# Two moves at the end of a decoder step: the transposition of the sampled parts' weights one slot later, and the last norm's spread written to two banks

## The chip, the cores and the metric

The kernel runs on one core of a Trainium2 chip. The metric is device microseconds of one execution, from the first instruction to the last transfer. Three executions of the kernel before took 937.68, 939.5 and 942.25 us, median 939.5 us. One further execution was profiled; it took 936.85 us.

The engines are named as the profile names them: PE multiplies matrices and writes its sums to banks of PSUM, DVE and ACT work on tiles and may read those banks, POOL works on tiles in SBUF, SP issues most transfers. Each engine works through its own instructions in their order and waits for others by semaphores.

## The reference

One step of a hybrid decoder on a prompt of 512 tokens and on 32 sampled tokens (8 sequences of 4). A first layer is a Mamba-2 mixer; a second is an attention mixer with three dilation groups that all read one shared K/V. What the change touches is the end of the second layer: the merging of the three groups' results by a softmax over their log-sum-exps, the gate, the output projection, the residual and the final norm.

```python
def dilated_mixer(h, attend, biases, g_norm, w_in, w_out):
    u = rmsnorm(h, g_norm) @ w_in
    q, gate = ...
    for g in range(N_DIL_GROUPS):
        o, lse = attend(q[:, :, g], biases[g], ...)
        ...
    w = jax.nn.softmax(jnp.stack(lses, axis=0), axis=0)
    o = jnp.sum(w[..., None] * jnp.stack(outs, axis=0), axis=0)
    y = o.reshape(b, l, ATT_WIDTH) * jax.nn.silu(gate)
    return y.astype(h.dtype) @ w_out

hp = hp + dilated_mixer(hp, attend_p, ...)      # the prompt
hs = hs + dilated_mixer(hs, attend_s, ...)      # the sampled tokens
y_prompt = rmsnorm(hp, final_norm)
y_sample = rmsnorm(hs, final_norm)
```

## The kernel before, in words

Prompt and sampled tokens stand side by side as 544 columns; the 1024 features are eight tiles of 128 rows. A product in full precision is made of three passes: operands are split into a high part (ACT) and a low part (DVE), and PE adds high x high, high x low and low x high. `mm` (line 146) and `transpose` (line 149) are the helpers through which nearly all PE work goes, so PE's rows are told apart by their tiles.

In the last stage a list of `units` is worked through: `attend(h, n)` for a head and a quarter of the prompt, `sample(h, q)` for a head and half of the sampled sequences, and near the end `combine()`. All three are generators; each `yield` ends one piece. Unit u's first piece is built in round u, its second in round u + 2, its third in u + 3, its fourth in u + 4, so other units' pieces stand between. After each round `run(n)` takes n matmuls from a `filler` that keeps PE busy with independent work: first the input projection for the queries and the gate (`pair_filler`, tiles `pa` and `pb`, inputs `bq`, weights `whi` and `wlo`), then the output projection (`out_proj`, inputs `yh` and `yl`, weights `wo`). The order in which instructions are built, with some marked urgent, is what a scheduler turns into the order on each engine; where an instruction lands in DVE's order thus follows from where it is built, and from what the scheduler puts ahead of it.

The gate's evacuation (`gate_evac`) is a chain through one spare tile `kv`: DVE L1213 reads the product's bank, ACT L1215 makes a Tanh, DVE L1220 (and L1222 for the sampled columns) and L1227 multiply, and ACT L1328 and DVE L1329 split the result into `yh` and `yl`. `wo` tiles are split by ACT L205 and DVE L206.

`combine` merges the sampled tokens' three groups. Piece one takes logarithms, transposes `lse`, makes the softmax in `qpad` (DVE L1484 to L1501, ACT L1496). Piece two transposes the weights on PE into the bank `lp2` (shown as `lp<-ident,qpad`), copies them to `sbt` (DVE L1507) and spreads them (L1508). Piece three makes sixteen small products `oc` in eight pairs, with two matmuls of the filler after each pair (`run(OCN)`, OCN is 2), and copies `oc` to `ys`, whose product with the gate is split last.

`out_proj` goes over the columns in two parts of 272 and over eight row tiles `m`; for each, 24 matmuls, then the residual (DVE L1610), a square (ACT L1611), a running sum (POOL L1613) and the gain (ACT L1614). When a part is done, its sums over the rows are made on PE (`ms`), and the reciprocal root is spread to all rows by a product of ones with a diagonal matrix (`rp`). For the last part `norm_last` does this: DVE multiplies six of the eight row tiles by the bank itself, in three pieces (L1592), each sent off by SP; ACT copies the bank to SBUF (L1585), POOL multiplies the other two tiles by that copy (L1588), and ACT's queue sends them (L1589).

Banks come from two pools in rotation: three for `pa` and `pb`, five (`pss`) for everything else here.

Of the kernel before, what the change touches and what calls it, by code (L numbers as in the profile page):

```python
# [127 lines left out]
def tile_yoco_step(  # L128
# [6 lines left out]
    nc = tc.nc  # L135
# [3 lines left out]
    def pin(ins):  # L139
        if pinned[0]:  # L140
            tc.keep_in_program_order(ins)
# [3 lines left out]
    def mm(*a, **k):  # L145
        pin(nc.tensor.matmul(*a, **k))  # L146

    def transpose(*a):
        pin(nc.tensor.transpose(*a))  # L149
# [7 lines left out]
    def half(name, dt=F32, shape=(128, 4, T)):  # L157
        return slab.tile(list(shape), dt, name=name, tag="s")

    def pj(name, cols=512):  # L160
        return psum.tile([128, cols], F32, name=name, tag="pj", bufs=3)

    def pss(name, shape=(128, 512)):
        return psum.tile(list(shape), F32, name=name, tag="ss", bufs=5)
# [15 lines left out]
    ones = const.tile([128, 128], F32, name="ones")  # L180
# [353 lines left out]
    for i in range(2):  # L534
        for j in range(2):
            p = pj("pa")
# [12 lines left out]
    dgs = tm[:, 1200:1584].rearrange("p (a b) -> p a b", b=128)  # L549
# [99 lines left out]
    def bc(ap, n):  # L649
        return ap[:, :, None].to_broadcast([ap.shape[0], ap.shape[1], n])  # L650
# [240 lines left out]
    def run(n):  # L891
        for _ in range(n):
            if next(fill, 0) == 0:
                return
# [237 lines left out]
    for k in range(4):  # L1132
        b1, b2 = (wk.tile([128, T], F32, name="hb", bufs=2) for _ in range(2))
# [343 lines left out]
    def combine():  # L1477
        nc.scalar.activation(lsm, lsm, AF.Ln)
        nc.vector.tensor_tensor(lse, lsm, lse, op=ALU.subtract)
        lp = pss("lp")  # L1480
        transpose(lp[0:16, 0:128], lse, ident)
        ltr = qpad[0][0:16]
        lt = ltr[:, 0:4, :]
        nc.vector.tensor_copy(lt.rearrange("p a b -> p (a b)"), lp[0:16, 0:128])  # L1484
        lv = lt[:, :, 0:12].rearrange("p j (g t) -> p j t g", t=TS)
        lgv = lt[:, :, 0:12].rearrange("p j (g t) -> p g j t", t=TS)
        red = ltr[:, 4, :].rearrange("p (a j t) -> p a j t", a=2, t=TS)
        mxg, sm_ = red[:, 0], red[:, 1]

        def all_groups(a):  # L1490
            return a[:, None, :, :].to_broadcast([16, 3, 4, TS])

        nc.vector.tensor_reduce(out=mxg, in_=lv, axis=AX.X, op=ALU.max)
        for g in range(3):
            nc.vector.tensor_tensor(lgv[:, g], lgv[:, g], mxg, op=ALU.subtract)
        nc.scalar.activation(lt[:, :, 0:12], lt[:, :, 0:12], AF.Exp)  # L1496
        nc.vector.tensor_reduce(out=sm_, in_=lv, axis=AX.X, op=ALU.add)
        nc.vector.reciprocal(sm_, sm_)
        for g in range(3):
            nc.vector.tensor_tensor(lgv[:, g], lgv[:, g], sm_, op=ALU.mult)  # L1500
        nc.vector.memset(lt[:, :, 12:32], 0.0)  # L1501
        yield
        lp2 = pss("lp2")
        transpose(lp2[:, 0:16], lt.rearrange("p a b -> p (a b)"), ident[0:16, 0:16])
        cmw = sbt[:, 0:272].rearrange("p (a b) -> p a b", b=16)
        ws, cm = cmw[:, 16, :], cmw[:, 0:16, :]
        nc.vector.tensor_copy(ws, lp2[:, 0:16])  # L1507
        nc.vector.tensor_tensor(cm, sel[:, None, :].to_broadcast([128, 16, 16]), bc(ws, 16), op=ALU.mult)  # L1508
        yield
        oc = pss("oc", (128, ATH, 2, 16))  # L1510
        for h in range(ATH):
            for q in range(2):
                mm(oc[:, h, q, :], o_s[:, q, h, :], cm[:, 2 * h + q, :], start=True, stop=True)
                if q:
                    run(OCN)
        nc.scalar.copy(y_s, oc.rearrange("p h q c -> p h (q c)"))
        sample_y()

    def sample_y():
        if len(late_smp) == 1:  # L1520
            nc.vector.scalar_tensor_tensor(y_s, y_s, 0.5, u_s, op0=ALU.mult, op1=ALU.mult)
            for i in range(2):
                split2(y_h[i][:, :, 0:NS], y_l[i][:, :, 0:NS], y_s[:, 4 * i:4 * i + 4, :])
        late_smp.append(1)
# [13 lines left out]
    def out_proj():  # L1538
        h2 = [half("h2"), half("h2")]
        for i in range(2):  # L1540
            dma(h2[i], h1d[:, 4 * i:4 * i + 4, :])
        e = half("e").rearrange("p a b -> p (a b)")
        accs, tmps = [e[:, HB * i:HB * i + HB] for i in range(2)], [e[:, HB * (2 + i):HB * (3 + i)] for i in range(2)]
        dgs = [e[:, HB * (4 + i):HB * (5 + i)] for i in range(2)]
        wos = {}

        def get(m):
            if m < KD and m not in wos:
                wos[m] = load_w(wo[m], half("wo", F32R, (128, 2, 8, 128)) if m < KD - 2 else None)

        def norm_sum(part, c0, c1):
            n = c1 - c0
            b0s = (0, 128, n - 128) if n > 256 else (0, 128)
            ms = pss("ms")
            for s_ in (0, 1):
                for b, b0 in enumerate(b0s):
                    mm(ms[:, b:b + 1], (accs, tmps)[s_][part if s_ == 0 else 1][:, b0:b0 + 128], inv_d,
                       start=s_ == 0 and b == 0, stop=s_ == 1, skip_group_check=True)
            return ms, n, b0s

        def norm_mul(sums, part, c0, c1):
            ms, n, b0s = sums
            rs = rstd_fin(ms, n, b0s, dgs[part])
            for m in range(0, KD, 2):
                hm = h2[m // 4][:, m % 4:m % 4 + 2, c0:c1]
                nc.vector.tensor_tensor(hm, hm, rs[:, None, 0:n].to_broadcast([128, 2, n]), op=ALU.mult)
                dma(yT[:, m:m + 2, c0:c1], hm)


        def norm_last(sums, part, c0, c1):  # L1570
            ms, n, b0s = sums
            sd = const.tile([128, 5], F32, name="sd", bufs=2)
            nc.scalar.activation(sd[:, 0:3], ms[:, 0:3], AF.Sqrt, bias=epst)
            nc.vector.reciprocal(sd[:, 0:3], sd[:, 0:3])
            idle = pss("idle")
            for _ in range(6):
                mm(idle[:, 0:128], ones, ones, start=True, stop=True)
            dg, rp = dgs[part], pss("rp")
            nc.scalar.activation(dg[:, 128:256], ident, AF.Copy, scale=sd[:, 1:2])
            nc.vector.tensor_scalar(dg[:, 0:128], ident, sd[:, 0:1], None, op0=ALU.mult)  # L1580
            nc.vector.tensor_scalar(dg[:, 256:n], ident[:, 384 - n:128], sd[:, 2:3], None, op0=ALU.mult)
            for b0, b1 in ((0, 128), (128, n)):
                mm(rp[:, b0:b1], ones, dg[:, b0:b1], start=True, stop=True, skip_group_check=True)
            rs = tmps[0][:, 0:n]
            nc.scalar.copy(rs, rp[:, 0:n])  # L1585
            for m in range(KD - 2, KD):
                hm = h2[m // 4][:, m % 4, c0:c1]
                nc.gpsimd.tensor_tensor(hm, hm, rs, op=ALU.mult)  # L1588
                nc.scalar.dma_start(yT[:, m, c0:c1], hm)  # L1589
            for m in range(0, KD - 2, 2):  # L1590
                hm = h2[m // 4][:, m % 4:m % 4 + 2, c0:c1]
                nc.vector.tensor_tensor(hm, hm, rp[:, None, 0:n].to_broadcast([128, 2, n]), op=ALU.mult)  # L1592
                dma(yT[:, m:m + 2, c0:c1], hm)

        get(0)
        parts = ((TH, T), (0, TH))
        for part, (c0, c1) in enumerate(parts):
            n = c1 - c0
            acc = accs[part]
            for m in range(KD):  # L1600
                get(m + 1)
                p = pj("pa")
                yield from proj_steps(p, [wos[m]], y_h, y_l, c0, c1, order=(0, 1, 2, 3, 5, 7, 6, 4))
                if part and m == 0:
                    sums = norm_sum(0, *parts[0])
                if part and m == 1:
                    norm_mul(sums, 0, *parts[0])
                hm = h2[m // 4][:, m % 4, c0:c1]
                sq = acc if m == 0 else tmps[m % 2]
                nc.vector.tensor_tensor(hm, p[:, 0:n], hm, op=ALU.add)  # L1610
                nc.scalar.activation(sq[:, 0:n], hm, AF.Square)  # L1611
                if 0 < m < KD - 1:
                    nc.gpsimd.tensor_tensor(acc[:, 0:n], acc[:, 0:n], sq[:, 0:n], op=ALU.add)  # L1613
                nc.scalar.activation(hm, hm, AF.Copy, scale=g_f[:, m:m + 1])  # L1614
        norm_last(norm_sum(1, *parts[1]), 1, *parts[1])

    ahead = [0]
# [130 lines left out]
```

## Time and profile before

| | |
|---|---|
| median of three runs | 939.5 us (937.68 to 942.25) |
| the profiled execution | 936.85 us, span 935.0 us |
| granted PE clock, mean | 0.995 |
| PE busy | 914.6 us, 98% of the span |
| DVE / ACT / POOL busy | 689.0 / 482.8 / 197.5 us |
| first output projection matmul | 873.34 us |
| last `rp` matmul ends | 928.29 us |

A row of a timeline gives start, duration, engine, line, operation and tiles (out<-in), and in brackets how long the engine had stood idle and what ended that. A row of a table by windows gives the stretch, its length, then the busy time and number of instructions of PE, PE's weight loads, DVE, ACT and POOL, then the granted PE clock (1.00 is full), the share of the DMA engines' time in use and GB/s. A row of waits gives the engine and tile that waited, for what, the total in us, how often, and the longest.

### The profile page before, as it was taken

How to read it: one execution, taken by the hardware profiler on the slowest of the kernel's cores; microseconds unless marked ns; L12 is line 12 of the kernel's file. 1: busy time of each engine (PE TensorE's matmuls, PEld its weight loads, DVE VectorE, ACT ScalarE, POOL GpSimd, SP SyncE). 2: the span in 40 equal slices, each digit the busy share in tenths (PEclk: the TensorE clock that was granted, in tenths of full speed). 3: DMA queues.
4: the chain of work that ended last, by engine and by line, in shares of the span. 5: the costliest groups of instructions: out<-in, count | busy, mean ns of one | idle time of the engine just before them, and what ended most of it. 6: DMA issues, size and time to landing. Idle time of an engine off the chain costs nothing.

```text
span 935.0 us, 21902 instructions
## 1 busy us (share of the span) xinstructions
PE 914.6 (98%) x8667; PEld 844.4 (90%) x8667; DVE 689.0 (74%) x1458; ACT 482.8 (52%) x1074; POOL 197.5 (21%) x295
## 2 busy tenths in 40 slices
PE   8999998999999999999999999999999999999996
PEld 8999887889888889999999999988888888888996
DVE  6997999989899889655489436866677766777732
ACT  6568655655655645322255213555555555557642
POOL 2133555644743733111101000000000000000021
PEclk9999999999999999999999999999999999999999
DMA  8225355255454443536287556767867868785411
GB/s 282 92 74 140 125 197 202 85 169 163 151 192 167 172 142 113 170 95 222 94 268 226 181 171 194 256 205 252 265 206 241 271 228 265 242 262 179 153 48 48
DMA packets 75950, 168.49 MB, mean 180 GB/s; under 512 B 19462, under 2 KB 37208, under 8 KB 75336
## 3 DMA queue, kind: packets, MB, share of 16 engines
q1 hardware_dynamic: 71464, 154.60, 50.3%
q10 hardware_dynamic: 3312, 9.75, 2.7%
q0 software_dynamic: 1072, 2.74, 1.1%
q8 instruction: 68, 1.11, 0.5%
q14 instruction: 34, 0.28, 0.1%
HBM read 141.14 MB, written 25.93 MB: 179 GB/s over the span
## 4 chain that ended last, share of the span: by engine, by line
PE 87%; DVE 5%; DMA 4%; ACT 2%; POOL 1%; issue 1%; SPq 0%; DVEq 0%; ACTq 0%
PE pa L146 35%; PE pb L146 30%; PE sp L146 3%; PE so L146 3%; PE pv L146 2%; PE s L146 2%; PE yd L146 1%; PE csp L146 1%; PE w L149 1%; PE ptp L149 1%; PE yo L146 1%; PE xp L149 1%; DMA ssmS<-s 1%; DVE co L638 1%; PE yos L146 1%; DMA kc<-ck 1%
## 5 line engine op out<-in xcount | busy, mean ns | idle before, releaser
L205 ACT ACTIVATE whi<-wraw 128x1024 fp32r<-128x1024 f32 x69 | 72.9, 1057 | 99.3 <-PE pb L146 68.7
L206 DVE TENSOR_TENSOR wlo<-wraw,whi 128x1024 fp32r<-128x1024 f32 x69 | 86.7, 1256 | 45.0 <-ACT whi L205 44.4
L146 PE MATMUL pa<-bq,whi 128*128 128x272 f32 x512 | 103.2, 296 | 0.0
L146 PE MATMUL pb<-nh,whi 128*128 128x288 f32 x280 | 83.7, 299 | 3.9 <-ACT cb L340 3.9
L146 PE MATMUL pb<-nl,whi 128*128 128x288 f32 x280 | 84.0, 300 | 0.0
L146 PE MATMUL pb<-nh,wlo 128*128 128x288 f32 x280 | 83.6, 299 | 0.0
L146 PEld LDWEIGHTS pa<-bq,whi 128*128 128x128 f32 x512 | 81.3, 189 | 0.9
L146 PE MATMUL pa<-nh,whi 128*128 128x256 f32 x280 | 80.6, 288 | 0.0
L146 PE MATMUL pa<-nl,whi 128*128 128x256 f32 x280 | 80.1, 286 | 0.0
L146 PE MATMUL pa<-nh,wlo 128*128 128x256 f32 x280 | 79.5, 284 | 0.0
L146 PE MATMUL pb<-bq,whi 128*128 128x272 f32 x384 | 77.1, 295 | 0.5 <-DVE kv L1213 0.5
L146 PE MATMUL pa<-bq,wlo 128*128 128x272 f32 x256 | 74.2, 290 | 0.0
L638 DVE SCALAR_TENSOR_TENSOR co<-cb,cvp,co 128x568 f32<-128x568 f32 x72 | 65.9, 917 | 0.8 <-ACT co L636 0.5
L146 PEld LDWEIGHTS pb<-bq,whi 128*128 128x128 f32 x384 | 60.8, 189 | 1.6 <-DVE kv L1213 0.8
L1449 POOL COPY lse<-mxs 128x1 f32<-128x1 f32 x16 | 4.6, 289 | 267.3 <-DVE mxs L1447 267.3
L1272 ACT ACTIVATE whi<-wraw 128x512 fp32r<-128x512 f32 x64 | 40.1, 626 | 36.8 <-PE pb L146 16.9
L146 PEld LDWEIGHTS pb<-nh,whi 128*128 128x128 f32 x280 | 53.1, 190 | 5.0 <-ACT cb L340 4.2
L146 PEld LDWEIGHTS pb<-nl,whi 128*128 128x128 f32 x280 | 53.0, 189 | 4.4 <-issue 4.4
L146 PE MATMUL pb<-bq,wlo 128*128 128x272 f32 x192 | 55.4, 289 | 0.0
L146 PEld LDWEIGHTS pb<-nh,wlo 128*128 128x128 f32 x280 | 53.1, 190 | 2.2 <-issue 2.2
L146 PEld LDWEIGHTS pa<-nh,whi 128*128 128x128 f32 x280 | 53.3, 190 | 1.9 <-issue 1.7
L146 PEld LDWEIGHTS pa<-nl,whi 128*128 128x128 f32 x280 | 53.3, 190 | 1.4 <-issue 1.4
(401 smaller groups left out, 2858.4 us busy)
## 6 DMA issues: line engine op xcount, KB each, us to landing
wraw<-w_in SPq DMA_DIRECT2D x40, 512.0 KB
kc<-ck SPq DMA_DIRECT2D x32, 640.0 KB
vc<-cv SPq DMA_DIRECT2D x32, 640.0 KB
wraw<-wb SPq DMA_DIRECT2D x32, 512.0 KB
s<-s SPq DMA_DIRECT2D x16, 512.0 KB
m<-aed SPq DMA_DIRECT2D x16, 512.0 KB
ssmS<-s ACTq DMA_DIRECT2D x16, 512.0 KB
wraw<-w_out SPq DMA_DIRECT2D x16, 512.0 KB
```

Of the source, the lines that this page charges most:

```text
L146: pin(nc.tensor.matmul(*a, **k))
L149: pin(nc.tensor.transpose(*a))
L205: a = nc.scalar.activation(hi, raw, AF.Copy)
L206: b = lo_eng.tensor_tensor(lo, raw, f32(hi), op=ALU.subtract)
L638: nc.vector.scalar_tensor_tensor(o, cb[:, k:k + n], cvp[:, ti, k:k + 1], o, op0=ALU.mult, op1=ALU.add)
L1272: nc.scalar.activation(hi, src[p][j], AF.Copy)
L1449: nc.gpsimd.tensor_copy(lse[:, i16:i16 + 1], mx[:, 2:3])
```

## The change

`combine` yields once more between its first and its second piece, so the transposition is built one round later, and with it all that follows in `combine`. In `norm_last` the spread is written twice, to a bank `rp` for DVE and to a bank `rc` for ACT; ACT copies from `rc`.

```diff
         nc.vector.memset(lt[:, :, 12:32], 0.0)
         yield
+        yield
         lp2 = pss("lp2")
         transpose(lp2[:, 0:16], lt.rearrange("p a b -> p (a b)"), ident[0:16, 0:16])
...
-            dg, rp = dgs[part], pss("rp")
+            dg, rp, rc = dgs[part], pss("rp"), pss("rc")
...
-            for b0, b1 in ((0, 128), (128, n)):
-                mm(rp[:, b0:b1], ones, dg[:, b0:b1], start=True, stop=True, skip_group_check=True)
+            for p in (rp, rc):
+                for b0, b1 in ((0, 128), (128, n)):
+                    mm(p[:, b0:b1], ones, dg[:, b0:b1], start=True, stop=True, skip_group_check=True)
             rs = tmps[0][:, 0:n]
-            nc.scalar.copy(rs, rp[:, 0:n])
+            nc.scalar.copy(rs, rc[:, 0:n])
```

What this does to the order. First PE, where the transposition was: it stood between the gate product `pa` of `bq_6930` and `pv` of the attention.

```order
 L146 MATMUL pa<-bq_6930,whi 128x272 x2
 L146 MATMUL pa<-bq_6930,wlo 128x272
-L149 MATMUL lp_11406<-ident,qpad_7044 128x16
 L146 MATMUL pv<-kv,pt 128x128 x2
 L146 MATMUL pv<-kv,pt 32x128 x4
```

It is now behind the attention's transposes `ptp`, and the rest of the gate products follow it without interruption. PE, some rows further, with the change (the products of `bq_6932` are the last of the gate's; `yh`, `yl` with `wo` are the output projection's first):

```order
L149 MATMUL ptp<-ident,s 32x128
L149 MATMUL lp_11453<-ident,qpad_7044 128x16
L146 MATMUL pb<-bq_6933,wlo 128x272
...
L146 MATMUL pa<-bq_6932,wlo 128x272
L146 MATMUL pa<-yh,wo 128x272
L146 MATMUL pa<-yl,wo 128x272
L146 MATMUL pa<-yh,wo 128x272 x2
L146 MATMUL oc<-sbt,os 128x16 x2
L146 MATMUL pa<-yl,wo 128x272
```

Before, the first `oc` stood directly behind `ptp`, and the eight pairs were spread over the last gate products; now they are spread over the first block of the output projection. The number of matmuls between them is the same.

Then DVE, at the copy and the spreading of the weights (L1507 and L1508 before, L1508 and L1509 with the change). With the change:

```order
L206 TENSOR_TENSOR wo<-wraw,wo 128x1024
L1220 SCALAR_TENSOR_TENSOR kv<-kv 128x272
L1329 TENSOR_TENSOR yl<-y_7037,yh 128x272
L1213 SCALAR_TENSOR_TENSOR kv<-pa,sums 128x272
L1227 SCALAR_TENSOR_TENSOR y_7037<-y_7037,kv 128x272
L1329 TENSOR_TENSOR yl<-y_7037,yh 128x384
L1508 COPY sbt<-lp_11453 128x16
L1220 SCALAR_TENSOR_TENSOR kv<-kv 128x240
L1222 SCALAR_TENSOR_TENSOR us<-kv 128x32
L1329 TENSOR_TENSOR yl<-y_7037,yh 128x272
L1227 SCALAR_TENSOR_TENSOR y_7037<-y_7037,kv 128x240
L1509 TENSOR_TENSOR sbt<-csts,sbt 128x256
```

Before, both stood fifteen rows and more higher, next to the attention's L1380, ahead of the last three gate evacuations; now the copy stands within the last evacuation (L1213 of `pa`, L1220, L1222, L1227) and the spreading behind it.

Last the end of the program on DVE, with the semaphores that each row waits for, before and with the change:

```order
L1592 TENSOR_TENSOR h_11510<-h_11510,rp 128x2x272 [waits Activation_49]
L1592 TENSOR_TENSOR h_11510<-h_11510,rp 128x2x272
L1592 TENSOR_TENSOR h_11511<-h_11511,rp 128x2x272
```

```order
L1594 TENSOR_TENSOR h_11487<-h_11487,rp 128x2x272 [waits PE_49]
L1594 TENSOR_TENSOR h_11487<-h_11487,rp 128x2x272
L1594 TENSOR_TENSOR h_11488<-h_11488,rp 128x2x272
```

DVE waited for ACT's copy of the same bank; now it waits for PE's last matmul into `rp`. On PE two matmuls into `rc` follow those into `rp`, and ACT's copy waits for them.

## The prediction

> **What bounds the kernel now.** I read the page first, then its chain of waits, then PE's waits, and only then the timelines of the stretch that the change touches.
>
> ```profile
> PE 914.6 (98%) x8667; PEld 844.4 (90%) x8667; DVE 689.0 (74%) x1458; ACT 482.8 (52%) x1074; POOL 197.5 (21%) x295
> PE 87%; DVE 5%; DMA 4%; ACT 2%; POOL 1%; issue 1%; SPq 0%; DVEq 0%; ACTq 0%
> ...
> PE lp L149 <- DVE qpad L1500: 0.7, 1, 0.7
> PE pb L146 <- DVE kv L1213: 0.5, 1, 0.5
> ...
> 879.37 22.15 PE pa L146 x176
> ```
>
> PE is busy 98% of the span, and 87% of the chain is PE. So a microsecond in which PE stands still costs a microsecond, and a microsecond saved on another engine is worth nothing unless PE waited for it. Of PE's waits, the one of 0.7 us is for `qpad` at L1500: that is the transposition of the weights, which the change moves. The other, 0.5 us for L1213, stands beside it. The last row, from the chain, gives the pitch of a 128x272 matmul, 22.15 / 176 = 0.126 us, and shows that after 879 us PE runs on without a gap, so whatever is lost or won before is carried to the end.
>
> **The transposition, what it removes.** PE and DVE in order of time, before the change:
>
> ```profile
> 861.89 0.29 PE L146 MATMUL pa<-bq,wlo 128*128 128x272 f32 x1
> 862.88 0.20 PE L149 MATMUL lp<-ident,qpad 16*128 16x16 f32 x1 [0.70 <-DVE qpad L1500]
> 863.01 1.07 PE L146 MATMUL pv<-kv,pt 128*128 128x128 f32 x12
> ...
> 869.02 0.29 PE L146 MATMUL pb<-bq,wlo 128*128 128x272 f32 x1
> ```
>
> Without `lp2` here `pv` would start one pitch after 861.89, at 862.02, and it starts at 863.01: 0.99 us are gained. Its inputs allow that: the copies into `pt` (L1391, L1392) are released by transposes before this place. One slot later `lp2` costs PE its own 863.01 - 862.88 = 0.13 us and no wait, as DVE finished `qpad` long before. Net -0.86 us. The 0.5 us for L1213 stays: that matmul adds to the bank that L1213 reads.
>
> **What the move puts in its place.** `oc`, the sixteen small products that use the weights, now begins four matmuls into the output projection, and its first one waits for DVE's L1509 (L1508 before), which spreads the transposed weights into `sbt`. DVE works in order, and L1509 now stands behind the last gate's evacuation. What stands ahead of it, and how long that took:
>
> ```profile
> 869.35 1.06 ACT L205 ACTIVATE wo<-wraw 128x1024 fp32r<-128x1024 f32 x1 [0.98 <-PE pb L146]
> ```
> ```profile
> 863.68 0.16 DVE L1507 COPY sbt<-lp 128x16 f32<-128x16 f32 x1
> 863.79 0.21 DVE L1380 TENSOR_SCALAR mx<-mx 128x1 f32<-128x1 f32 x1
> 863.92 0.42 DVE L1508 TENSOR_TENSOR sbt<-csts,sbt 128x256 f32<-128x256 f32 x1
> ...
> 870.44 1.23 DVE L206 TENSOR_TENSOR wo<-wraw,wo 128x1024 fp32r<-128x1024 f32 x1 [0.30 <-ACT wo L205]
> 871.58 0.43 DVE L1220 SCALAR_TENSOR_TENSOR kv<-kv 128x272 f32<-128x272 f32 x1
> 871.94 0.43 DVE L1329 TENSOR_TENSOR yl<-y,yh 128x272 fp32r<-128x272 f32 x1
> 873.53 0.44 DVE L1213 SCALAR_TENSOR_TENSOR kv<-pa,sums 128x272 f32<-128x272 f32 x1 [1.17 <-PE pa L146]
> ...
> 875.60 0.40 DVE L1227 SCALAR_TENSOR_TENSOR y<-y,kv 128x240 f32<-128x240 f32 x1
> 875.92 0.42 DVE L1521 SCALAR_TENSOR_TENSOR ys<-ys,us 128x256 f32<-128x256 f32 x1
> ```
>
> The clock for all of it is the end of the last `pb` product, 869.02 + 0.29 = 869.31. From there:
>
> - ACT's L205 splits the second `wo` tile, and DVE's L206 begins at 870.44: 1.13 us later.
> - L206, L1220, L1329 take 871.58 - 870.44 = 1.14, then 0.36, and about 0.35 for the next of the same form, so L1213 can begin 1.85 us after L206. Before, it waited 1.17 us more for PE; now PE is early, and DVE is what is late.
> - From L1213 to the end of L1227, 875.92 - 873.53 = 2.39 us (in it an ACT Tanh that waits for L1227 and is waited for by L1220). L1508 adds 0.11 (863.79 - 863.68), L1509 0.42.
>
> Sum: 1.13 + 1.85 + 2.39 + 0.11 + 0.42 + 0.03 for the semaphore = 5.93 us after that end. PE reaches the first `oc` much sooner: twelve matmuls of the last gate product and four of the projection follow, so its next start would be 869.02 + 17 x 0.126 = 871.16, or 1.85 us after the same end. PE loses 5.93 - 1.85 = 4.08 us, shown as a wait of about 3.9, since a last matmul's 0.29 us end is drawn past its pitch. Behind that `oc` all of PE stands, the rest of the projection included. The eight pairs of `oc` and sixteen matmuls between them are as many as before. Later covers hold: the split of the third `wo` tile follows the end of the first projection block, as before, so it moves with PE.
>
> Bounds: if ACT's L205 or DVE's L206 kept their old place in time the wait would be shorter by the 0.98 us that ACT waited for PE; I take 3.1 as the low end. If every DVE hand-over costs 0.03 us more, ten of them, 4.4. I take 4.08. Stretch: -0.86 + 4.08 = +3.2 us.
>
> **The clock behind the wait.** The trace holds one wait of that length, at 160.5 us, and shows what follows it. Windows, with the granted clock behind the five engines, and PE's rows:
>
> ```profile
> 164.40:165.00 0.60, 0.55 (x4) 0.55 (x5) 0.60 (x2) 0.60 (x4) 0.60 (x1) 1.00 0.00 0
> 165.00:165.50 0.50, 0.50 (x5) 0.50 (x5) 0.47 (x3) 0.26 (x1) 0.50 (x3) 0.86 0.00 0
> 165.50:166.00 0.50, 0.50 (x4) 0.50 (x3) 0.50 (x1) 0.35 (x1) 0.50 (x2) 0.50 0.00 0
> 168.50:168.75 0.25, 0.25 (x3) 0.25 (x3) 0.25 (x2) 0.25 (x2) 0.09 (x1) 0.50 0.00 0
> 168.75:169.00 0.25, 0.25 (x3) 0.13 (x1) 0.25 (x1) 0.25 (x3) 0.00 (x0) 0.95 0.00 0
> 933.25:933.50 0.25, 0.00 (x0) 0.00 (x0) 0.00 (x0) 0.00 (x0) 0.00 (x0) 0.73 0.98 357
> ```
> ```profile
> 160.23 0.28 PE L146 MATMUL pa<-nh,wlo 128*128 128x256 f32 x1
> 164.45 0.40 PE L146 MATMUL pb<-nh,whi 128*128 128x288 f32 x1 [3.94 <-ACT cb L340]
> 164.69 0.30 PE L146 MATMUL pb<-nl,whi 128*128 128x288 f32 x1
> 164.82 0.29 PE L146 MATMUL pb<-nh,wlo 128*128 128x288 f32 x1
> 166.06 0.45 PE L146 MATMUL pb<-nh,whi 128*128 128x288 f32 x1
> 166.30 0.45 PE L146 MATMUL pb<-nl,whi 128*128 128x288 f32 x1
> ```
>
> About 0.9 us after PE had resumed, the clock went to 0.50 at 165.36 (0.86 = 1 - 0.28 / 2 of that row) and came back at 168.77: 3.41 us at half, in which a matmul came every 0.24 us where 0.13 stood before. The drop at the end, at 933.36, lies 768.0 us later, 225 x 3.413, so such windows follow a fixed beat. The one that brought the first drop, 161.95 to 165.36, was 27% busy; the one from 926.53 to 929.95, half busy up to the last `rp` near 928.3, brought none. A wait of 3.9 us leaves one of its windows at best 43% busy, at some phases empty. So I expect a drop in most executions. At half rate the 3.41 us lose up to 1.7 us; where the drop falls inside the wait, part of it is lost on an idle PE, down to 0.7. I take 1.4, bounds 0 and 3.4 (two windows).
>
> The Trainium skill (TensorE: Matmul & The Clock Gate, section "What's actually happening") says that half rate is what PE falls to after at least one idle window of about 3.4 us. The length agrees with the 3.41 measured here; that the window must be idle does not, since the one at 161.95 was 27% busy. Read strictly, it would let a wait of 3.9 us drop the clock in about (3.9 - 3.41) / 3.41, one phase in seven, and the time would be that of the second rival below.
>
> **The last norm's spread.**
>
> ```profile
> 928.37 0.39 ACT L1585 COPY e<-rp 128x272 f32<-128x272 f32 x1 [1.06 <-PE rp L146]
> 928.79 1.98 DVE L1592 TENSOR_TENSOR h<-h,rp 128x544 f32<-128x544 f32 x3 [1.45 <-ACT e L1585]
> 928.83 1.48 POOL L1588 TENSOR_TENSOR h<-h,e 128x272 f32<-128x272 f32 x2 [5.46 <-ACT e L1585]
> 929.54 1.67 SPq L1593 DMA_DIRECT2D yT<-h  x3
> 927.81 0.48 PE rp L146 x4
> 930.25:930.50 0.25, 0.00 (x0) 0.00 (x0) 0.25 (x1) 0.00 (x0) 0.06 (x1) 1.00 0.21 74
> 930.50:930.75 0.25, 0.00 (x0) 0.00 (x0) 0.25 (x1) 0.00 (x0) 0.00 (x0) 1.00 1.00 357
> ```
>
> DVE's three multiplications waited for ACT's copy out of the same bank; with a bank of its own DVE waits for `rp` alone and starts at about 928.37, 0.42 us earlier. The second spread, `rc`, is as many rows again, 0.48 us (row of the chain), so the copy and POOL start 0.48 us later. That is covered: from 930.4 to past 933.25 the DMA engines are full with the results, so what counts is when the first transfer starts, and that is SP's at 929.54, which follows DVE's first piece. POOL's two small parts then come at about 930.1 and 930.8 (928.83 + 0.48, and 0.74 for each), while the queues are still full. Gain 0.42 us; bounds 0 (POOL's last part ends all) and 0.45.
>
> **The sum.** +3.2 + 1.4 - 0.4 = +4.2 us. The profiled execution took 936.85 us for a span of 935.0, so 941.0 us. It lies 2.65 us under the median of the runs shown, 939.5; against that median the forecast is 939.5 + 4.2 = 943.7 us, or +0.44%. About 0.5%, 4.7 us, is what a measurement of this kernel can tell from no change.
>
> **The rivals.**
>
> 1. *Slower beyond doubt: the clock stays down for two windows.* Where the beat splits the wait in the middle, both windows hold about 1.95 us of it, and the second may keep the clock low too. For it: the 27% row. Against: after 164.45 one busy window was enough. Price +3.2 + 3.4 - 0.4 = +6.2 us, 945.7; it passes 0.5% once more than 1.9 us go to the clock.
> 2. *The wait, but no drop.* For it: the half-busy window near 928. Against: the drop at 165.36. +3.2 - 0.4 = +2.8 us, 942.3.
> 3. *Not slower: PE never waits for L1509.* If DVE were done by the time PE is there, only the gains stand: -0.86 - 0.42 = -1.3 us, 938.2. For it: DVE is 74% busy, and has 1.17 us of slack ahead of L1213. Against: the sum above, 5.93 against 1.85; DVE would have to be 4 us ahead of every row quoted.
> 4. *The second bank does nothing*, because POOL's late start ends the run: the sum is 0.4 us higher, 944.1. The full DMA rows speak against it.
>
> **How the numbers follow.** Forecast (one drop) 55%, rival 1 15%, rival 2 17%, rival 3 4%, rival 4 9%. The likeliest gives 943.7. The runs of before lie 4.6 us apart, so a median can be off by some 1.5 us: low 940.5 (rival 2 less that), high 947 (rival 1 plus it). Slower by over 0.5%: a third of the forecast (0.19), most of rival 1 (0.13), a little of 2, and half of rival 4 (0.04), 0.38 in all. Faster by over 0.5%: 0.02. Within: 0.60.
>
> **What would show it.** In the new profile: no wait of PE for `qpad`; one wait of PE of 3.5 to 4.3 us at `oc`, for DVE `sbt` L1509, near 870 us; behind it a window of 3.41 us at clock 0.5; DVE's L1594 starting with `rc`, no longer behind ACT. If there is no wait at `oc`, the middle part is wrong; if it is there and the clock stays at 1.00, the clock term is; if the first result transfer does not start about 0.4 us sooner after the last `rp`, the last part is.

## The result and the profile after

The changed kernel takes 947.95 us (median of five executions, 945.6 to 950.35) against 939.5 us before (five executions beside it, 937.55 to 942.25): a ratio of 1.0096, 95% interval 1.0077 to 1.0116. It is slower by 8.4 us, where +4.2 was forecast, and above the upper end of the range, 947. The profiled execution took 947.61 us for a span of 945.8, against 936.85 and 935.0.

First the new wait of PE in the changed kernel (engine and tile, what it waited for, total us, times, longest):

```profile
PE oc L146 <- DVE sbt L1509: 3.9, 1, 3.9
```

The wait for `qpad` is gone from the list and one of 3.9 us stands in its place, as the prediction had it. DVE's and PE's timelines show how it comes about, and how long the stage then lasts:

```profile
870.42 1.23 DVE L206 TENSOR_TENSOR wo<-wraw,wo 128x1024 fp32r<-128x1024 f32 x1 [0.30 <-ACT wo L205]
...
872.27 0.44 DVE L1213 SCALAR_TENSOR_TENSOR kv<-pa,sums 128x272 f32<-128x272 f32 x1
...
874.64 0.42 DVE L1509 TENSOR_TENSOR sbt<-csts,sbt 128x256 f32<-128x256 f32 x1
```
```profile
857.76 0.28 PE L149 MATMUL lp<-ident,lse 128*16 128x128 f32 x1
...
869.00 0.29 PE L146 MATMUL pb<-bq,wlo 128*128 128x272 f32 x1
...
870.86 0.41 PE L146 MATMUL pa<-yh,wo 128*128 128x272 f32 x2
875.21 0.76 PE L146 MATMUL oc<-sbt,os 128*128 128x16 f32 x4 [3.94 <-DVE sbt L1509]
...
876.41 0.87 PE L146 MATMUL oc<-sbt,os 128*128 128x16 f32 x4
877.71 0.87 PE L146 MATMUL oc<-sbt,os 128*128 128x16 f32 x4
...
890.39 0.27 PE L149 MATMUL op<-ident,on 128*128 128x128 f32 x1
```

From the end of the last `pb` product, 869.29, the first `oc` starts 5.92 us later; 5.93 was worked out. What was not foreseen is the pitch behind it: one step of the alternation (two `oc` products, shown as four instructions, and two matmuls of the projection) takes 877.71 - 876.41 = 1.30 us. Before, the same step took 0.70 us:

```profile
856.20 0.28 PE L149 MATMUL lp<-ident,lse 128*16 128x128 f32 x1
...
867.76 0.52 PE L146 MATMUL oc<-sbt,os 128*128 128x16 f32 x4
868.45 0.51 PE L146 MATMUL oc<-sbt,os 128*128 128x16 f32 x4
...
879.10 0.27 PE L149 MATMUL op<-ident,on 128*128 128x128 f32 x1
```

The windows of the changed kernel, cut at the beat of 3.413 us, show why (after the stretch and its length: busy time and instructions of PE, its weight loads, DVE, ACT and POOL; then the granted clock):

```profile
872.08:875.49 3.41, 0.28 (x3) 0.31 (x3) 3.27 (x11) 1.15 (x3) 0.00 (x0) 1.00 0.53 157
875.49:878.91 3.42, 3.42 (x17) 3.42 (x17) 0.12 (x1) 0.00 (x0) 0.00 (x0) 0.50 0.00 1
878.91:882.32 3.41, 3.41 (x18) 3.41 (x17) 0.00 (x0) 0.00 (x0) 0.00 (x0) 0.50 0.00 0
882.32:885.73 3.41, 3.41 (x16) 3.41 (x17) 0.17 (x1) 0.37 (x1) 0.00 (x0) 0.50 0.00 0
885.73:889.15 3.42, 3.42 (x22) 2.81 (x21) 1.10 (x4) 1.43 (x5) 0.00 (x0) 0.50 0.00 0
889.15:892.56 3.41, 3.41 (x29) 3.41 (x29) 2.67 (x3) 3.02 (x4) 0.00 (x0) 1.00 0.11 18
```

The clock is at half for four windows, 13.65 us, and not for one. PE is drawn busy all through them, and its waits show nothing there: only the granted clock and the pitch tell of the loss. In the kernel before, the same mix of products ran at full clock:

```profile
868.51:871.93 3.42, 3.42 (x31) 3.42 (x31) 2.72 (x5) 2.12 (x4) 0.00 (x0) 1.00 0.44 156
```

**Where the 10.8 us of the two spans lie.** From the transposition of `lse` to the last `op` the kernel before took 879.10 - 856.20 = 22.90 us, the changed one 890.39 - 857.76 = 32.63: 9.73 us more. Of these the stretch is 3.2 by the forecast, so 6.5 go to the clock; half of 13.65 would be 6.8. (The run with the covered wait, below, measures the stretch without a drop, and leaves 6.3.) Ahead of `lse`, where the change touches nothing, the profiled execution after ran 857.76 - 856.20 = 1.56 us late. The rest is a gain at the end, in PE's, DVE's and SP's rows:

```profile
938.81 0.64 PE L146 MATMUL rp<-e,ones 128*128 128x128 f32 x4
939.28 0.63 PE L146 MATMUL rc<-e,ones 128*128 128x128 f32 x4
939.49 1.98 DVE L1594 TENSOR_TENSOR h<-h,rp 128x544 f32<-128x544 f32 x3 [0.98 <-PE rp L146]
...
940.28 1.62 SPq L1595 DMA_DIRECT2D yT<-h  x3
```

DVE starts 0.68 us after the first `rp`, no longer behind ACT. Before, it started 1.15 us after it (928.79 against `rp` at 927.64, in a row quoted further down), so 0.47 us are won there. The first result transfer starts 1.47 us after `rp` instead of 1.90 (929.54 in the prediction), and to the end of the span it is 945.8 - 938.81 = 7.0 us instead of 7.4.

### The profile page after: what moved, and what is told of

Its sections match the earlier page's. It is cut to its first block, busy times and chain, and to the rows that moved or that the text cites. A ratio compares the mean times of both kernels' runs of the same rounds, so it can differ in the third digit from the quotient of the medians.

```text
span 945.8 us, 21909 instructions
## 1 busy us (share of the span) xinstructions
PE 923.0 (98%) x8671; PEld 852.0 (90%) x8671; DVE 687.5 (73%) x1458; ACT 483.5 (51%) x1074; POOL 196.7 (21%) x295
## 4 chain that ended last, share of the span: by engine, by line
PE 87%; DVE 5%; DMA 3%; ACT 2%; issue 1%; POOL 1%; SPq 0%; POOLq 0%; DVEq 0%; ACTq 0%
PE pa L146 35%; PE pb L146 30%; PE sp L146 3%; PE so L146 3%; PE s L146 2%; PE pv L146 2%; PE yd L146 1%; PE csp L146 1%; PE yo L146 1%; PE ptp L149 1%; PE xp L149 1%; PE w L149 1%; PE yos L146 1%; DVE co L638 1%; DMA kc<-ck 1%
```

## The experiments

**Two theories on the four windows.** Theory 1: the clock is kept down by what runs behind the wait. The `oc` products pass 16 columns for each load of 128x128 weights, so little passes through the array while PE is drawn busy; behind the wait of 160 us, on which the forecast was modelled, only wide products follow. Theory 2: the number of windows follows from the wait itself, its length or its place on the beat. A third question is whether the whole loss comes from the late place of the spread L1509 in DVE's order. In all diffs the changed kernel is the starting point unless something else is said.

### One part alone: the transposition

```diff
-            dg, rp, rc = dgs[part], pss("rp"), pss("rc")
+            dg, rp = dgs[part], pss("rp")
...
-            for p in (rp, rc):
-                for b0, b1 in ((0, 128), (128, n)):
-                    mm(p[:, b0:b1], ones, dg[:, b0:b1], start=True, stop=True, skip_group_check=True)
+            for b0, b1 in ((0, 128), (128, n)):
+                mm(rp[:, b0:b1], ones, dg[:, b0:b1], start=True, stop=True, skip_group_check=True)
...
-            nc.scalar.copy(rs, rc[:, 0:n])
+            nc.scalar.copy(rs, rp[:, 0:n])
```

> The transposition one slot later, the last spread in one bank as before. If the whole loss comes from the place of the transposition: the change with both parts measured +8.4 us over the kernel before (947.95 against 939.5), its second part is priced at -0.4, so +8.8 us, about 948.3, with PE's wait of 3.9 us at the first oc, and behind it about 13.6 us at half clock. If the second spread bank were part of the loss: less than +8 us.

Measured: 946.69 us against 938.0, ratio 1.0087 (1.0055 to 1.012), +8.7 us by the medians. The wait is 3.9 us again. In the profiled execution the clock stays down for five windows, 878.35 to 895.42; before them the end of the wait, then the first and the fourth:

```profile
874.94:878.35 3.41, 0.18 (x2) 0.00 (x0) 3.41 (x11) 1.09 (x4) 0.00 (x0) 1.00 0.62 207
878.35:881.77 3.42, 2.72 (x12) 2.75 (x13) 0.96 (x3) 0.40 (x1) 0.00 (x0) 0.50 0.00 1
...
888.59:892.01 3.42, 3.42 (x20) 2.81 (x21) 0.42 (x1) 1.14 (x4) 0.00 (x0) 0.50 0.00 0
```

So the loss is the transposition's, as far as these intervals tell. Here the wait lies otherwise on the beat: the first `oc`, at 879.05, starts 0.70 us behind the drop, in the change (875.21) 0.28 us ahead of it. The number of windows is five instead of four. Both theories allow that: by theory 1, the last of the alternation, at 888.33 in this execution, and the products of `pv` behind it run into a fourth window (888.59 to 892.01), and only the fifth is full of wide products.

### The other part alone: the second bank

The kernel before with the two banks, without the added `yield`.

> The last norm's spread in two banks alone; the transposition at its old place. By the prediction's term -0.42 us, bounds 0 and -0.45: 0.04% of the time, less than a comparison of this kernel can tell, so the profile has to show it: from the start of the last rp products to the end of the span 7.0 us instead of 7.36, DVE's L1593 starting with the second bank's products instead of behind ACT's copy. If POOL's later start ends the run: 7.4 us, no gain.

Measured: 936.33 us against 939.29, ratio 0.9979 (0.9959 to 0.9998). The profile:

```profile
926.80 0.64 PE L146 MATMUL rp<-e,ones 128*128 128x128 f32 x4
927.47 1.98 DVE L1593 TENSOR_TENSOR h<-h,rp 128x544 f32<-128x544 f32 x3 [0.98 <-PE rp L146]
```
```profile
927.64 0.63 PE L146 MATMUL rp<-e,ones 128*128 128x128 f32 x4
```

The second fence is the kernel before: from `rp` to the end of the span 935.0 - 927.64 = 7.4. With the second bank it is 933.8 - 926.80 = 7.0, as expected. Of the 2.0 us that the ratio gives the profiles explain only some 0.4; the interval reaches down to 0.2, and the executions of the kernel before in this comparison lie between 935.86 and 944.83. The sign agrees with the term, the size beyond 0.4 is not shown.

### Taking the cause of the wait away

The copy and the spread of the weights stand earlier in DVE's order; the transposition stays one slot later.

```diff
-        nc.vector.tensor_copy(ws, lp2[:, 0:16])
-        nc.vector.tensor_tensor(cm, sel[:, None, :].to_broadcast([128, 16, 16]), bc(ws, 16), op=ALU.mult)
+        with tc.high_priority():
+            nc.vector.tensor_copy(ws, lp2[:, 0:16])
+            nc.vector.tensor_tensor(cm, sel[:, None, :].to_broadcast([128, 16, 16]), bc(ws, 16), op=ALU.mult)
```

> The change, with the copy and the spread of the weights into sbt (L1508, L1509) ahead in DVE's order, behind the evacuation of the second last gate and in front of the second split of wo instead of behind the whole last evacuation. If the wait at the first oc is the only thing wrong with the new place: no wait there, no drop of the clock, the two gains of the prediction alone remain, -0.86 and -0.42, about 938.2. If pushing L1414 and L1329 back by 0.5 us makes PE wait elsewhere: up to 0.5 us more, 938.7. If the drop needs no wait but only the oc products at the new place: +5 us, about 945.

> The same kernel as the one with the early copy and spread, in more rounds. Its first comparison gave 0.9991 (0.9975 to 1.0007), the sum of the two gains would be -1.28 us, 0.9986. The profile gave -0.71 us between the transposition of lse and the last op, where -0.86 was expected. With -0.37 at the end: -1.1 us, about 0.9988. If a new wait elsewhere eats it: 1.0000.

Measured: 937.47 against 938.0, ratio 0.9991 (0.9975 to 1.0007), and in more rounds 937.29 against 939.29, ratio 0.9976 (0.9956 to 0.9997). PE in the first of the two:

```profile
860.56 0.28 PE L149 MATMUL lp<-ident,lse 128*16 128x128 f32 x1
...
873.92 0.51 PE L146 MATMUL oc<-sbt,os 128*128 128x16 f32 x4
874.61 0.51 PE L146 MATMUL oc<-sbt,os 128*128 128x16 f32 x4
...
882.75 0.27 PE L149 MATMUL op<-ident,on 128*128 128x128 f32 x1
```

No wait, a pitch of 0.69, and from `lse` to the last `op` 22.19 us instead of 22.90: the gain of 0.86 that the prediction worked out for the old place is there, to within 0.15 (the profile of the second comparison gives 876.57 - 854.36 = 22.21). The `oc` products at their new place, among the projection, do not by themselves pull the clock down. So in the profiles the move of the transposition is worth 0.7 us, and the change lost because DVE's two instructions moved with it. This kernel is clearly faster than the changed one. Against the kernel before, the second comparison makes it a little faster and the first can't tell the two apart; nor can it be told from the second bank alone (0.9979).

### Covering the wait

Fifteen products of ones ahead of the first `oc` give PE work while DVE is as late as before.

```diff
         oc = pss("oc", (128, ATH, 2, 16))
+        idle = pss("idle")
+        for _ in range(15):
+            mm(idle[:, 0:128], ones, ones, start=True, stop=True)
```

> The change, with fifteen products of ones put in front of the first oc (result unused, about 0.24 us each, 3.6 us in all), so that PE works through the time in which it waited for L1509; the path of DVE is as late as before. Theory 1, that the idle stretch starts the drop: the clock stays at 1.00, only the stretch of 3.2 us less 0.4 remains, +2.8 us, about 942.3. Rival, that the small oc products themselves, at their new place among the projection, pull the clock down, wait or no wait: about 13 us at half clock again, +8.4 us or more, about 948.

Measured: 941.87 against 938.0, ratio 1.0035 (1.0011 to 1.0059). The profiled execution:

```profile
858.42 0.28 PE L149 MATMUL lp<-ident,lse 128*16 128x128 f32 x1
...
875.87 0.59 PE L146 MATMUL oc<-sbt,os 128*128 128x16 f32 x4 [0.59 <-DVE sbt L1509]
876.64 0.51 PE L146 MATMUL oc<-sbt,os 128*128 128x16 f32 x4
...
884.77 0.27 PE L149 MATMUL op<-ident,on 128*128 128x128 f32 x1
```

The pitch is 0.77 for the step with the wait's end and 0.70 behind it, and the clock stays at 1.00. The first `oc` starts 5.92 us behind the end of the last `pb` product, as in the change, so in this stretch the two profiles differ only in the products of ones and in the clock. From `lse` to the last `op` it takes 884.77 - 858.42 = 26.35 us: 3.45 more than before, which is the stretch (3.2 was worked out), and 6.28 less than the change, which is the clock. The times of the runs agree less closely: 0.35% of 938.0 is +3.3 us, the stretch less the gain at the end (+2.8 expected), so some 5 of the change's 8.4 us are left for the clock. The ten executions spread from 937.8 to 947.87, and their mean clocks from 0.998 to 0.986; the clock seems to have dropped in some of them too, but none of those was profiled.

Then half of the cover, seven products instead of fifteen:

> The change, with seven products of ones in front of the first oc instead of fifteen: 7 x 0.234 = 1.64 us of the wait covered, about 2.3 us of it left. A window of 3.41 us that holds all of it is 33% busy, one that holds half is 66% busy. If a window must be less than about a third busy to drop the clock (27% did at 161.95, and about half did not at 926.53): a drop in few executions, +2.8 us in the others. If any wait of 2 us drops it: +8 us or more, with four or five windows, as in the change.

Measured: 948.67 against 939.29, ratio 1.0101 (1.0061 to 1.0141); all four executions between 947.65 and 949.82. The wait is 2.4 us. The window in which it lies, and the first at half clock:

```profile
874.15:877.56 3.41, 1.05 (x10) 1.08 (x10) 2.63 (x9) 1.15 (x3) 0.00 (x0) 1.00 0.43 137
877.56:880.98 3.42, 3.42 (x18) 3.42 (x18) 0.00 (x0) 0.00 (x0) 0.00 (x0) 0.50 0.00 0
```

My expectation of a drop in few executions was a miss: the window before the drop was 31% busy here, and the clock fell, for four windows (877.56 to 891.22). A wait that is 1.5 us shorter bought nothing. As the windows are as many as with 3.9 us, theory 2 is not helped by the length of the wait.

### Other work behind the same wait

36 of the projection's 272-column products behind the first pair of `oc` products, the other pairs after them.

```diff
                 if q:
-                    run(OCN)
+                    run(OCN if h else 36)
```

> The change, with 36 of the projection's 272-column products behind the first pair of oc products instead of two; the other seven pairs come after them, all products are computed. The wait of 3.9 us stays. Theory 1, that the clock is kept down by what runs behind the wait (small products alternating with large ones): the first window that is full of 272-column products lifts it, one or two windows of 3.41 us instead of four, so 3.4 to 5.1 us less than the change: 942.9 to 944.5. Theory 2, that the number of windows follows from the length or phase of the wait alone: 13.65 us at half clock as in the change, about 948.

Measured: 944.96 against 938.0, ratio 1.0061 (1.0038 to 1.0083), +7.0 us by the medians, 0.5 us above the upper end of what was expected. The interval overlaps that of the change, so the profile has to tell. The wait is the same 3.9 us. The windows:

```profile
872.29:875.70 3.41, 0.19 (x2) 0.00 (x0) 3.41 (x11) 1.11 (x4) 0.00 (x0) 1.00 0.55 195
875.70:879.12 3.42, 2.70 (x12) 2.73 (x13) 0.98 (x3) 0.40 (x1) 0.00 (x0) 0.50 0.02 6
879.12:882.53 3.41, 3.41 (x17) 3.41 (x16) 0.35 (x1) 0.00 (x0) 0.00 (x0) 0.50 0.00 0
882.53:885.94 3.41, 3.41 (x31) 3.41 (x30) 1.32 (x2) 1.79 (x3) 0.00 (x0) 1.00 0.00 0
```

Two windows, 6.83 us. The first window that is full of wide products, 879.12 to 882.53, lifts the clock, and the seven `oc` pairs that then follow run at a full clock. The wait has the same length as in the change, and this execution's drop comes 0.72 us ahead of the end of its wait, as in the run with five windows (0.70). So length and place on the beat are those of the run with five windows, and there are two: theory 2 falls.

### Wider products, same weights

Each `oc` product passes 128 columns instead of 16. The first 16 are the wanted ones; the others are written over by the next product, or not read.

```diff
-        oc = pss("oc", (128, ATH, 2, 16))
+        oc = pss("oc")
         for h in range(ATH):
             for q in range(2):
-                mm(oc[:, h, q, :], o_s[:, q, h, :], cm[:, 2 * h + q, :], start=True, stop=True)
+                c = 16 * (2 * h + q)
+                mm(oc[:, c:c + 128], o_s[:, q, h, :], sbt[:, c:c + 128], start=True, stop=True, skip_group_check=True)
...
-        nc.scalar.copy(y_s, oc.rearrange("p h q c -> p h (q c)"))
+        nc.scalar.copy(y_s, oc[:, 0:256].rearrange("p (h c) -> p h c", h=ATH))
```

> The change, with each oc product 128 columns wide instead of 16: as many products, the same weights loaded, the first 16 columns of each are the wanted ones and the others are written over by the next product. The wait of 3.9 us stays. At full clock a 128x128 product of ones took 0.117 us in the kernel with the covered wait, and an oc instruction took 0.112 (0.70 for four, less two matmuls of 0.126), so the alternation costs nearly the same. Theory 1a, that what keeps the clock down is that few columns pass through the array for each load of weights: the clock comes back after one or two windows of 3.41 us, +4.5 to +6.2 us over the kernel before. Theory 1b, that the alternation itself does it (change of weights, bank or type at every step): four or five windows, +8 to +9.5 us.

Measured: 943.26 against 939.29, ratio 1.0046 (1.0027 to 1.0064), +4.0 us, 0.5 below the lower end of theory 1a's sum and half of theory 1b's. PE's rows and the window at the beat:

```profile
879.64 1.05 PE L146 MATMUL oc<-sbt,os 128*128 128x128 f32 x4
880.94 1.03 PE L146 MATMUL oc<-sbt,os 128*128 128x128 f32 x4
882.07 0.61 PE L146 MATMUL oc<-sbt,os 128*128 128x128 f32 x4
882.76 0.61 PE L146 MATMUL oc<-sbt,os 128*128 128x128 f32 x4
```
```profile
878.42:881.83 3.41, 3.41 (x18) 3.41 (x18) 0.00 (x0) 0.00 (x0) 0.00 (x0) 0.50 0.00 0
881.83:885.24 3.41, 3.41 (x33) 3.29 (x36) 0.03 (x1) 0.37 (x1) 0.00 (x0) 1.00 0.00 0
```

The steps take as long as with 16 columns, 1.30 us at half clock and 0.69 at full: the 112 columns more cost nothing. But the clock comes back in the midst of the alternation, after two windows, 875.00 to 881.83. The beat lies otherwise here than in the change: the drop comes 1.89 us ahead of the first `oc` (876.89), so the first of the two windows is in good part the rest of the wait. The second is full of the alternation, and it lifts the clock; in the change three such windows with 16 columns did not. The number of products, the weights, the wait and the time of a step are the same; only the columns differ. That is theory 1a, and the alternation as such (1b) is excluded.

### Small products without any wait

The kernel with the early copy and spread, all `oc` products in one stretch, and that stretch run twice. The diff is against that kernel.

```diff
-        for h in range(ATH):
+        for h in 2 * list(range(ATH)):
             for q in range(2):
                 mm(oc[:, h, q, :], o_s[:, q, h, :], cm[:, 2 * h + q, :], start=True, stop=True)
-                if q:
-                    run(OCN)
+        for h in range(ATH):
+            run(OCN)
```

> The kernel with the early copy and spread (no wait at oc), but all sixteen oc products in one stretch, and that stretch run twice over (the second time writes the same values again), the projection's sixteen products behind it. TensorE has work throughout: about 16 x 0.45 = 7.2 us of 16-column products, 3.6 us more work than before, so at least one whole window of 3.41 us holds nothing else. Theory 1b, one measure for drop and return, the columns that pass in a window: the alternation passes 3.41 / 0.70 x 608 = 2960 at full clock (it held the clock) and 1580 at half (it kept it down), this stretch only about 480, so the clock drops in the midst of it though TensorE never waits, for one to three windows: early spread + 3.6 + 2 to 5 us, about +5 to +8 over the kernel before. Theory 2b, that a drop needs an idle stretch of TensorE, and small products only fail to lift it: no drop, early spread + 3.6, about +2.5.

Measured: 944.42 against 936.44, ratio 1.0092 (1.0043 to 1.0141), +8.0 us, the upper end of theory 1b's sum. (1b is here the idea that one count of columns decides over drop and return, not the alternation as in the run before.) PE has no wait at `oc`:

```profile
871.81 9.72 PE L146 MATMUL oc<-sbt,os 128*128 128x16 f32 x64
```
```profile
872.72:876.14 3.42, 3.42 (x33) 3.42 (x32) 1.49 (x4) 0.00 (x0) 0.00 (x0) 1.00 0.45 153
876.14:879.55 3.41, 3.41 (x18) 3.41 (x17) 0.00 (x0) 0.00 (x0) 0.00 (x0) 0.50 0.00 0
...
886.38:889.79 3.41, 3.41 (x28) 3.41 (x29) 1.22 (x2) 2.56 (x4) 0.00 (x0) 1.00 0.02 5
```

The window from 872.72 to 876.14 is 100% busy, and the clock drops at its end all the same, for three windows. No idle time is needed: 33 instructions of 16 columns in a window do it. Theory 2b falls with this run.

The same trace shows that the place on the beat counts too. At the wait of 160 us, behind which only wide products follow, this execution's clock fell in the midst of the wait, 1.68 us ahead of its end at 164.43, and stayed down for two windows:

```profile
162.75:166.17 3.42, 1.74 (x7) 1.74 (x8) 3.38 (x6) 2.42 (x7) 3.34 (x5) 0.50 0.28 109
166.17:169.58 3.41, 3.41 (x17) 3.40 (x16) 3.11 (x5) 1.62 (x6) 2.39 (x5) 0.50 0.00 0
```

The first of them, half of it the rest of the wait, left the clock down; the one full of wide products lifted it. The other ten profiles have one window there.

## Why the prediction was wrong

**What held.** The old place: 0.86 us to gain; with the wait taken away, 0.71 measured. The wait: 5.93 us behind the last `pb` worked out, 5.92 measured; shown as 3.94 where about 3.9 was said. That it agrees to 0.01 is luck: the copy L1508, put at 0.11, lengthens nothing (from L1213 to L1509 it is 874.64 - 872.27 = 2.37 us, the copy in it), and from the end of L1509 to the `oc` 0.15 us pass where 0.03 was put for the semaphore, a term that no run shows. The stretch of +3.2: 3.45 with the covered wait, at full clock. The last spread: -0.42 worked out, about -0.4 in the profiles. The rival that PE would never wait, and the one that the second bank does nothing, are excluded by the profiles.

**What failed is one term, the clock:** "I take 1.4, bounds 0 and 3.4 (two windows)". Measured: 6.3 us against the covered wait (6.5 with the forecast's stretch), four windows in the profiled execution, five in the one with the transposition alone. With that size the forecast's own sum gives 3.2 + 6.3 - 0.4 = +9.1, and the medians +8.4, within the spread of the runs. The drop at the beat behind the wait was right; its length was taken over from the wait at 160.5 us without asking what runs behind each wait. There, 288-column products follow, and one window of them lifted the clock. Here, the alternation with 16-column products follows for 8 x 1.30 = 10.4 us. The trace of before held the rows for it: the `oc` instructions take nearly as long as the matmuls around them (0.112 us against 0.126) and pass 16 columns. Even the upper bound, two windows, was too small by half. The first rival came nearest, but its reason for a second window, "where the beat splits the wait in the middle", is what the last run shows at the wait of 160 us (162.75 to 169.58), and not what held the clock down for four here, since all four begin behind the wait's end.

The prediction also calls the drop at 165.36 the first. The trace of before has an earlier one, at 49.31, behind a window that is 40% busy with products on 32 of the array's 128 columns; seven of the eleven profiled executions have it. So even before the change a busy share of 27% was not the largest at which the clock fell.

**One count orders most of these windows.** Columns that pass in 3.41 us, worked out from the pitches or counted in the rows:

| what runs | columns | what the clock did |
|---|---|---|
| `oc` alone, full clock: 3.41 / 0.112 x 16 | 490 | fell |
| alternation at half clock: 3.41 / 1.30 x 608 | 1,590 | stayed down |
| the fourth of the five windows, 888.59 to 892.01, with the transposition alone | 2,260 | stayed down |
| the 27% busy window at 161.95: 0.92 / 0.13 x 288 | 2,040 | fell |
| 926.53 to 929.95 of the kernel before: sixteen products of 128 and 144 columns | at most 2,080 | stayed up |
| 162.25 to 165.66 of the kernel with the early copy: nine products of 288 | at most 2,590 | fell |
| alternation of 128 columns at half clock: 3.41 / 1.30 x 1,056 | 2,770 | came back |
| alternation at full clock: 3.41 / 0.70 x 608 | 2,960 | stayed up |
| 288-column products at half clock: 3.41 / 0.24 x 288 | 4,090 | came back |

(608 is two matmuls of 272 and four instructions of 16; 1,056 has four of 128. The window at 161.95 and the pitch of 0.24 are in the prediction. The window at 888.59 holds seven matmuls of 272 columns, two of 128 and two of 16 on the whole array, and eight of 128 on 32 rows by 32 columns, a sixteenth of it: 1,904 + 256 + 32 + 8 x 128 / 16 = 2,256. Counted without the share of the array it would be 3,216, and would not fit.) A line near 2,600 or 2,700 columns (the edges of a window leave a product or two uncertain) would explain both why the alternation holds a clock that is up and why it did not lift one that is down: at half clock it passes about half as much. But that the chip counts just this isn't shown, and two kinds of windows don't fit. The one from 926.53 lies far below the line and stayed up:

```profile
926.53:929.95 3.42, 1.75 (x16) 1.53 (x14) 1.77 (x5) 0.92 (x3) 1.12 (x2) 1.00 0.00 0
```

Its products are in plain f32 and take longer for each column (0.117 us for 128 columns of ones in the covered wait, 0.126 for 272 in the projection); counted double they would fit. And with the transposition alone, the window from 830.56 to 833.98, mostly products on 32 of the array's columns, passes 4,480 columns, or 1,150 by their share of the array, and stayed up, while the one from 663.31 to 666.72, with 4,620 and 910, fell. No run varied the type or the share of the array alone.

The Trainium skill (TensorE: Matmul & The Clock Gate, section "What's actually happening") gives full rate after at least one busy window of about 3.4 us, and half rate after at least one idle one, on a beat that runs by itself. The beat agrees: the times at half clock behind the waits above are multiples of 3.413 us (6.83, 10.24, 13.65, 17.07). The two conditions differ from what was measured, if busy is read as the profile draws it: three windows of the change drawn as 100% busy (875.49 to 885.73) did not lift the clock, and one drawn so (872.72 to 876.14 of the last run) let it fall.

**What stays open.** Why some executions with the covered wait were as slow as the change (one at 947.87) was not seen in a profile. How far the executions of one kernel differ in windows, four or five, is known from one profile each. What count of work the clock goes by, for drop and for return, is open, as said above.

## What to carry to other kernels

Before pricing a wait of PE, look at what runs behind it: if the next ten microseconds are products with few columns for each load of weights, a drop of the clock may last not one window but four or five, as here, and cost more than the wait. When a piece of work is moved to a later slot, move back by hand what another engine must have done for it (here that was two DVE instructions of 0.5 us together, and with them ahead again the loss was gone). Wide products first behind the wait brought two windows instead of four or five, but only 1.4 us by the medians. A PE that is drawn 100% busy can run at half its rate; read the granted clock and the pitch beside the busy share.

## What the runs showed of the hardware

That a small product costs as much as a wide one with the same weights: four `oc` instructions and two matmuls took 0.69 to 0.70 us with 16 columns and with 128, at full clock, and 1.30 at half.

That the clock falls under work without a wait: behind the window from 872.72 to 876.14 of the last run, 100% busy with 16-column products.

That the share of busy time alone does not decide: in the run with the transposition alone, a further drop came at 666.72, behind this window:

```profile
663.31:666.72 3.41, 1.93 (x29) 0.69 (x23) 0.09 (x2) 0.37 (x1) 0.00 (x0) 1.00 0.61 207
```

It is 57% busy, with products on 32 of the array's 128 columns and waits for a transfer between them. The window from 926.53 to 929.95 of the kernel before, 51% busy and with full-width products, brought no drop. That the share of the array counts too, as in the table's window at 888.59, is one reading of these windows; the window from 830.56, 54% busy and with much the same products, brought no drop either, and it was not tested by itself.
